# A two-layer encoder on one core: bonus products issued behind the next unit's lta, small weights loaded earlier, one projection block moved forward

## The chip, the core and the metric

The kernel runs on one core of a Trainium2 chip. A core has a matrix engine (TensorE, PE in the profile), a vector engine (VectorE, DVE), an activation engine (ScalarE, ACT), a general engine (GpSimd, POOL) and a sync engine (SyncE, SP) whose queue issues most DMA transfers; ACT's own queue issues some too. Each engine works through its instructions in program order, and the engines wait for each other by semaphores. The metric is the device time of one execution in microseconds (us); lower is better.

## The reference

A sequence of 1280 tokens (one prompt of 256, one sample of 1024) with 1024 channels passes two layers. Layer 0 mixes tokens with a bidirectional RWKV-7 scan, layer 1 with neighbourhood attention; each is followed by a squared-ReLU MLP with 4096 hidden channels. The part that matters here is the preparation of the scan in layer 0:

```python
xw, xa = h + xx * mix[3], h + xx * mix[4]
r, k, v = (h + xx * mix[i]) @ w_rkv[i]      # i = 0, 1, 2
kk = l2_normalised_per_head(k * k_k)
for d in range(2):                          # forward, backward
    w_lora = tanh(xw @ w1[d]) @ w2[d]
    decay = exp(-exp(-softplus(-(w0[d] + w_lora)) - 0.5))
    iclr = sigmoid(a0[d] + (xa @ a1[d]) @ a2[d])
    k_d = k * (1 + (iclr - 1) * k_a)
    y += wkv_scan(r, decay, k_d, v, -kk, kk * iclr, reverse=(d == 1))
    bonus += sum_over_head(r * k_d * r_k)
...
y = groupnorm(y) + bonus * v
out = (y * g) @ w_o
```

All data is float32. The large products are computed as three matmuls each, on operands split into a rounded high part and a rest (high x high, high x low, low x high).

## The kernel before

Channels are tiled in eight blocks of 128, tokens in three segments of 256, 512 and 512. Layer 0 is one stretch of code, `l0_proj`, in these steps.

*Projections.* The norm, the token mixes and the products with `w_k` and with block 0 of `w_r` (receptance) are done first; the results `k_d` and `r_d` go to DRAM. The last result of this step is copied out of PSUM by ACT (L308, kt) and stored by SP (L309).

*Prep stage.* There are 48 units h = 6m + 2s + d, for channel block m, segment s and direction d; the even units are the forward ones. Unit after unit, the following is done:

- `prep_first` (L602): two small matmuls with 64 rows, ltw (decay) and lta (learning rate), from the small weights `wa` of the block. Forward units use the first 64 rows, backward ones the last 64. Each writes a PSUM tile, two buffers of each kind. ACT applies tanh and scalings (L606, L598, L610, L611).
- `prep_scan` (L621, DVE), `prep_exp` (L629 and L632, ACT) and `prep_products` (L649, L655, L663 and L667 on POOL; L651, L657, L659 and L661 on DVE). L657 and L661 read the unit's lta tile last, and with L661 done its bank is free; the ltw bank is free when the scan has read it.
- `prep_keys`, even units only: a 16-row matmul of `heads` (head indicators) with the key norms `kr` into PSUM tile kb (L678), then L681 on DVE.
- `prep_bonus`, even units only: step 0 is a DVE product (L693) that waits for POOL's sum of the two directions (L667), step 1 the bonus matmuls of two columns each, written into the unit's old kb tile (L697), step 2 four DVE copies from there (L703). The next keys matmul but one needs that tile again and waits for the copies.
- `prep_weights`: `wa` of a block, a transfer that ACT's queue issues (L590). `prep_load` (L586): SP loads k (pk), and r of block 0 (pr).

Between these small pieces TensorE is given large work: in blocks 1 to 7 the receptance of the block to come (rps, L96 to L98 by way of `rmm`), and from unit 42 on the values (vps, `v_block`, L516 to L518). Their weights are loaded by SP (`wraw`, L394), cast by ACT (L399) and split by POOL (L400). ACT takes the results out of PSUM (L419 into pr, L522 into vt); both kinds of result share two PSUM buffers. The mixed input of the values is loaded by SP (`vload`, L435), cast by ACT (`vcut`, L439) and split by DVE or POOL (`vlo`, L445).

*What sets the order.* TensorE, DVE, ACT and POOL carry out exactly the order of a list: each piece is put in with a time in units of h, and the list is sorted by it. `lead(t)` stands for max(h + t, -1 + 0.01 h), so that the pieces of the first units gather at -1. A weight's load is at t - 1.988 and its cast at t, both with lower limits. Only SP's queue is ordered by the program's scheduler. At time 52 the scan stage begins, whose first pieces (L837, and L865 copying mt) are mixed in with the last value matmuls. After that come layer 0's output and MLP, the attention layer and its MLP, which take most of the time.

The two lines that set the bonus and the lta in the order:

```python
            at(lead(-0.9), self.prep_first, U, h, 1)
...
                for i, t in enumerate((2.5, 3.0, 3.2)):
                    at(h + t, self.prep_bonus, U, h, i)
```

In unit h, then, the ltw of unit h + 5 comes at h + 2.973, the bonus matmuls of unit h at h + 3.0 and the lta of unit h + 4 at h + 3.1.

Of the kernel before, what the change touches and what calls it, by code (L numbers as in the profile page):

```python
# [5 lines left out]
F32 = mybir.dt.float32  # L6
# [7 lines left out]
P = 128  # L14
# [37 lines left out]
class Trunk:  # L52
# [48 lines left out]
    def l0_proj(self):  # L101
        nc, tc, a = self.nc, self.tc, self.a
# [11 lines left out]
        lp = lctx.enter_context(tc.tile_pool(name="lpA", bufs=1, side="right", reuse_waits="tile"))  # L114
        pre = self.pre = {nm: lp.tile([P, T], F32, name=nm) for nm in ("tw", "ta")}
        pre["kr"] = lp.tile([96, 512], F32, name="kr")
        hctx = ExitStack()
        hp = hctx.enter_context(tc.tile_pool(name="hp", bufs=1, side="right"))
        wk = hctx.enter_context(tc.tile_pool(name="wkA", bufs=2, side="right"))
# [5 lines left out]
        h = hp.tile([P, KT, W], F32, name="h")  # L125
# [65 lines left out]
        def mix_tiles():  # L191
            return [tuple(Pieces(mixp, f"{x}{k}") for x in ("mh", "ml")) for k in range(KT)]
# [154 lines left out]
        while extra:  # L347
            extra.pop(0)()

        w = [self.wsplit(wp, a["w_r"][m], 1024, nc.gpsimd, hb=3, rb=1) for m in range(1)]  # L350
        for s in range(3):
            need(0, s)
# [10 lines left out]
        U = [{} for _ in range(48)]  # L363
        N = 48
        self.cq = []
        at = lambda t, f, *x: self.cq.append((t, len(self.cq), lambda: f(*x)))
        for h in range(N):
            lead = lambda t: max(h + t, -1.0 + 0.01 * h)
            at(lead(-4.633), self.prep_load, U, h)
            at(lead(-2.027), self.prep_first, U, h, 0)  # L370
            at(lead(-0.9), self.prep_first, U, h, 1)
            at(lead(-1.765), self.prep_first, U, h, 2)
            at(lead(-0.65), self.prep_keys, U, h, 0)
            at(lead(-0.2), self.prep_keys, U, h, 1)
            at(lead(-1.1), self.prep_scan, U, h)
            at(lead(-0.693), self.prep_exp, U, h, 0)
            at(lead(-0.69), self.prep_exp, U, h, 1)
            for i, t in enumerate((0.084, 0.415, 0.517, 0.53, 0.54, 0.55, 0.56, 0.57)):
                at(h + t, self.prep_products, U, h, i)
            at(h + 1.191, self.prep_store, U, h, nc.sync)  # L380
            if h % 2 == 0:
                for i, t in enumerate((2.5, 3.0, 3.2)):
                    at(h + t, self.prep_bonus, U, h, i)
            if h % 6 == 0:
                at(max(h + -6.0, -1.5), self.prep_weights, h // 6)
            if h % 6 == 0 and h < 24:
                for i, t in enumerate((0.4, 2.4, 3.4)):
                    at(h + t, self.prep_sigmoid, h // 6, i)
# [12 lines left out]
            wq[key] = hi, lo  # L401

        def weight(key, src, t):
            at(max(t - 1.988, -1.9), wraw, key, src)
            at(max(t, -1.0), wcut, key)
        ev = {}

        def rmm(m, s, k):
# [11 lines left out]
        RL = 4.5  # L420
        for m in range(1, 8):
            for j in range(2):
                weight(("r", m, j), a["w_r"][m, :, 512 * j:512 * j + 512], 6 * m - RL - 2.0 + 0.3 * j)
            for s in range(3):
                for k in range(KT):
                    at(6 * m + 2 * s - RL + 0.25 * k - 0.4, rmm, m, s, k)
                at(6 * m + 2 * s - RL + 1.6, rev, m, s)

        act, vx = mix_tiles(), {}
        VM = 43.3  # L430

        def vload(k, s):
            c0, c1 = SEGS[s]
# [12 lines left out]
        for i, (s, k) in enumerate((s, k) for s in range(3) for k in range(KT)):  # L446
            t = VM + 2 * s - 4 + 0.2 * k
            at(t - 1.9, vload, k, s)
            at(t, vcut, k, s)
            at(t + 0.35, vlo, k, s)  # L450
        VS, VD, VL = 42.5, 0.62, 0.8
        vt = lambda i: VS + VD * i

        def vmm(i):
# [6 lines left out]
        for q in range(4):  # L461
            for j in range(4):
                weight(("v", q, j), a["w_v"][q, :, 2 * j:2 * j + 2, :].rearrange("p k c -> p (k c)"), max(vt(10 * q) - 2.32 + 0.3 * j, vt(10 * q - 1) + 0.01 * j if j > 1 and q else -2.0))
# [64 lines left out]
    def prep_open(self, bctx):  # L528
        nc, tc, a = self.nc, self.tc, self.a
        self.ar_d = self.dram("ar_d", [8, 2, P, 20, P])  # L530
        self.bk_d = self.dram("bk_d", [8, 2, P, 20, P])
        pp = self.pp = bctx.enter_context(tc.tile_pool(name="ppB", bufs=1, reuse_waits="tile", side="right"))
        self.pk = bctx.enter_context(tc.tile_pool(name="pkB", bufs=2, reuse_waits="tile", side="right"))
        self.ppl = bctx.enter_context(tc.tile_pool(name="plB", bufs=2, space=PSUM))
        self.ppn = bctx.enter_context(tc.tile_pool(name="pnB", bufs=2, space=PSUM))
        s = self.pre
        s["ec"] = [[pp.tile([P, 8, 65], F32, name=f"ec{d}{i}") for i in range(2)] for d in range(2)]
        s["raw"] = pp.tile([P, 640], F32, name="l2raw")
        s["m64"] = pp.tile([P, 512], F32, name="m64")
        nc.sync.dma_start(s["m64"], a["m64"])  # L540
        s["hw"] = pp.tile([P, 48], F32, name="hw")
        s["heads"] = pp.tile([96, 1024], F32, name="heads")
        nc.sync.dma_start(s["heads"], a["heads"][0:96])

    def prep_const(self):
        nc, s = self.nc, self.pre
# [242 lines left out]
    def at(self, t, f, level=3):  # L789
        self.todo.append((t, len(self.todo), f, level))  # L790
# [1312 lines left out]
```

## Time and profile before

| | us |
|---|---|
| median of three runs | 3968.65 |
| lowest and highest | 3967.81, 3971.26 |
| the profiled execution | 3964.76 |
| its span | 3963.0 |
| prep stage within the span | about 282 to 645 |

The profile is of one execution. Its granted TensorE clock is 0.977 on average. A row of a timeline gives start and duration in us, engine, line, operation, the tiles out<-in, sizes and how many like it were merged; in brackets stands how long the engine had been idle before it and what ended that. One float32 matmul of the small kind shows as two records, two passes over its columns. A row of windows gives the stretch, its length, the busy time of PE, weight loads, DVE, ACT and POOL, the granted clock, the share of the DMA engines and GB/s.

### The profile page before, as it was taken

What the parts mean: (1) busy time and instruction counts of PE and PEld (TensorE: products, weight loads), DVE (VectorE), ACT (ScalarE), POOL (GpSimd) and SP (SyncE); (2) the same over time, 40 slices, a digit from 0 to 9 for tenths busy, and PEclk for the clock granted to TensorE, in tenths of its full rate; (3) what the DMA queues carried; (4) which work ended last, traced back from release to release, by engine and by line L of the source; (5) the groups of instructions that cost most, each with busy time, mean ns of one, the idle gap of its engine ahead of it and who ended that gap; (6) DMA issues with size and microseconds to landing.
All of it is one profiled execution on the core that took longest, in us unless ns stands there. A gap on an engine that the chain in (4) does not pass through costs nothing.

```text
span 3963.0 us, 89877 instructions
## 1 busy us (share of the span) xinstructions
PE 3751.8 (95%) x36484; PEld 3150.9 (80%) x36484; DVE 2368.9 (60%) x4441; ACT 1684.4 (43%) x4129; POOL 1691.5 (43%) x1541
## 2 busy tenths in 40 slices
PE   8989999888888899999999999999989999999999
PEld 5755579778888788888888889887778788888888
DVE  5777743656565446666666682355563656666666
ACT  6786652555555532222222242456663222222222
POOL 4446652122222424555555561344442455555554
PEclk9989999999999899999999999999999999999999
DMA  3235565666664430111111115444455111111111
GB/s 137 71 105 217 206 227 153 161 164 154 161 152 117 138 115 32 43 40 38 38 43 40 43 64 161 115 108 109 102 146 182 43 35 43 43 41 43 38 40 62
DMA packets 459375, 393.53 MB, mean 99 GB/s; under 512 B 268400, under 2 KB 353520, under 8 KB 458960
## 3 DMA queue, kind: packets, MB, share of 16 engines
q1 hardware_dynamic: 438368, 368.36, 32.3%
q10 hardware_dynamic: 20592, 19.41, 1.5%
q8 instruction: 288, 4.72, 0.5%
q14 instruction: 127, 1.04, 0.1%
HBM read 269.85 MB, written 123.78 MB: 99 GB/s over the span
## 4 chain that ended last, share of the span: by engine, by line
PE 67%; DVE 7%; DMA 5%; ACT 4%; issue 3%; POOL 1%; SPq 1%; ACTq 0%; DVEq 0%; POOLq 0%
PE ps L96 12%; PE ps L97 12%; PE ps L98 12%; PE ps L1491 4%; PE ps L1492 4%; PE ps L1493 4%; PE wu L1009 4%; PE vps L516 1%; PE vps L517 1%; PE vps L518 1%; PE aps L1009 1%; PE op L2015 1%; PE kps L1009 1%; DVE q L878 1%; PE lps L1009 1%
## 5 line engine op out<-in xcount | busy, mean ns | idle before, releaser
L96 PE MATMUL ps<-ah,whi 128*128 128x512 f32 (+1 forms) x2304 | 842.9, 366 | 4.3 <-ACT whi L90 3.3
L98 PE MATMUL ps<-ah,wlo 128*128 128x512 f32 (+1 forms) x2304 | 824.8, 358 | 4.7 <-POOL wlo L91 3.9
L97 PE MATMUL ps<-al,whi 128*128 128x512 f32 (+1 forms) x2304 | 826.2, 359 | 0.0
L96 PEld LDWEIGHTS ps<-ah,whi 128*128 128x128 f32 x2304 | 435.0, 189 | 79.6 <-issue 9.2
L98 PEld LDWEIGHTS ps<-ah,wlo 128*128 128x128 f32 x2304 | 434.0, 188 | 77.4 <-POOL wlo L91 4.5
L97 PEld LDWEIGHTS ps<-al,whi 128*128 128x128 f32 x2304 | 435.2, 189 | 65.6 <-issue 1.0
L1495 DVE TENSOR_TENSOR x<-ps,x 128x512 f32<-128x512 f32 x784 | 484.6, 677 | 0.0
L1399 POOL TENSOR_TENSOR rl<-rl 128x512 f32<-128x512 f32 (+1 forms) x192 | 174.0, 906 | 630.4 <-ACT rl L1398 352.0
L1398 ACT ACTIVATE rl<-ps 128x512 f32<-128x512 f32 (+1 forms) x192 | 101.1, 526 | 793.2 <-PE ps L98 793.2
L91 POOL TENSOR_TENSOR wlo<-raw,whi 128x1024 fp32r<-128x1024 f32 (+1 forms) x113 | 232.8, 2061 | 216.9 <-ACT whi L90 184.0
L1491 PE MATMUL ps<-hhTrue,dh 128*128 128x512 f32 x784 | 307.4, 392 | 1.7 <-DVE x L1495 1.7
L1492 PE MATMUL ps<-hlTrue,dh 128*128 128x512 f32 x784 | 307.4, 392 | 0.0
L1493 PE MATMUL ps<-hhTrue,dl 128*128 128x512 f32 x784 | 306.9, 391 | 0.5 <-POOL dl L1383 0.5
L1383 DVE TENSOR_TENSOR hlTrue<-ts,hhTrue 128x512 fp32r<-128x512 f32 x112 | 133.0, 1187 | 150.0 <-ACT hhTrue L1382 150.0
L1383 POOL TENSOR_TENSOR dl<-raw,dh 128x512 fp32r<-128x512 f32 x128 | 208.8, 1643 | 9.5 <-ACT dh L1382 8.5
L90 ACT CAST whi<-raw 128x1024 fp32r<-128x1024 f32 (+1 forms) x141 | 132.4, 939 | 184.5 <-PE ps L97 77.3
L1506 DVE TENSOR_TENSOR x<-ps,x 128x512 f32<-128x512 f32 x224 | 148.7, 685 | 95.2 <-PE ps L98 93.9
L1383 DVE TENSOR_TENSOR hlTrue<-rl,hhTrue 128x512 fp32r<-128x512 f32 x98 | 88.7, 908 | 185.0 <-ACT hhTrue L1382 184.8
L1382 ACT CAST dh<-ds 128x512 fp32r<-128x512 f32 x112 | 69.3, 619 | 278.5 <-POOL ds L1446 278.5
L1383 POOL TENSOR_TENSOR dl<-ds,dh 128x512 fp32r<-128x512 f32 x112 | 159.1, 1421 | 63.5 <-ACT dh L1382 63.5
L1952 POOL TENSOR_TENSOR s<-s,mx 128x384 f32<-128x384 f32 (+1 forms) x150 | 110.1, 747 | 163.0 <-DVE mx L1951 121.3
L1493 PEld LDWEIGHTS ps<-hhTrue,dl 128*128 128x128 f32 x784 | 147.2, 188 | 33.6 <-POOL dl L1383 1.4
(339 smaller groups left out, 10262.3 us busy)
## 6 DMA issues: line engine op xcount, KB each, us to landing
raw<-in_w_down_dram SPq DMA_DIRECT2D x128, 256.0 KB, 2.8
raw<-in_w_up_dram SPq DMA_DIRECT2D x64, 512.0 KB, 3.4
ar<-ar_d SPq DMA_DIRECT2D x80, 256.0 KB, 3.5
bk<-bk_d SPq DMA_DIRECT2D x80, 256.0 KB, 3.6
ar_d<-ar SPq DMA_DIRECT2D x32, 512.0 KB, 2.7
bk_d<-bk SPq DMA_DIRECT2D x32, 512.0 KB, 3.4
bs<-tab SPq DMA_DIRECT2D x128, 96.0 KB, 3.9
v_d<-vt ACTq DMA_DIRECT2D x80, 128.0 KB, 3.6
```

Of the source, the lines that this page charges most:

```text
L91: lo_eng.tensor_tensor(out=lo[:, cs], in0=raw, in1=hi[:, cs].bitcast(F32), op=ALU.subtract)
L96: mm(ps, sh, mh, start=first, stop=False)
L97: mm(ps, sh, ml, start=False, stop=False)
L98: mm(ps, sl, mh, start=False, stop=last)
L1009: self.nc.tensor.matmul(out, w, x, start=start, stop=stop, skip_group_check=free)
L1383: eng.tensor_tensor(out=lo, in0=src, in1=hi.bitcast(F32), op=ALU.subtract)
L1399: nc.gpsimd.tensor_tensor(out=r, in0=r, in1=r, op=ALU.mult)
L1491: mm(ch[j], hi[:, cs], hh, start=bool(new), stop=False, skip_group_check=True)
L1492: mm(ch[j], hi[:, cs], hl, start=False, stop=False, skip_group_check=True)
L1493: mm(ch[j], lo[:, cs], hh, start=False, stop=True, skip_group_check=True)
L1495: nc.vector.tensor_tensor(out=xv, in0=ch[j], in1=xv, op=ALU.add)
L1506: nc.vector.tensor_tensor(out=xv, in0=ps, in1=xv, op=ALU.add)
```

## The change

- The bonus steps go from (2.5, 3.0, 3.2) to (2.6, 3.12, 3.3). The keys' steps go from -0.65 and -0.2 to -0.55 and -0.15.
- The tiles `heads` and `wa` of block 0 move into a pool that is open earlier, and SP loads them ahead of the first `w_r` block; `prep_weights` is left out for unit 0.
- The limits on weight loads and casts go from -1.9 and -1.0 to -2.3 and -2.2. Block 1's receptance weights are cast at -2.1, and its matmuls and copies are due 5.4 units ahead (4.5 before, and still so in blocks 2 to 7).
- The values' loads, casts and splits come 0.3 units earlier (VM), their copies out of PSUM 0.1 earlier (VL).

```diff
+        pre["heads"] = lp.tile([96, 1024], F32, name="heads")
+        pre["wa", 0] = lp.tile([P, 2, P], F32, name="wa0")
...
+        nc.sync.dma_start(pre["wa", 0], a["wa2"][0])
+        nc.sync.dma_start(pre["heads"], a["heads"][0:96])
         w = [self.wsplit(wp, a["w_r"][m], 1024, nc.gpsimd, hb=3, rb=1) for m in range(1)]
...
-            at(lead(-0.65), self.prep_keys, U, h, 0)
-            at(lead(-0.2), self.prep_keys, U, h, 1)
+            at(lead(-0.55), self.prep_keys, U, h, 0)
+            at(lead(-0.15), self.prep_keys, U, h, 1)
...
-                for i, t in enumerate((2.5, 3.0, 3.2)):
+                for i, t in enumerate((2.6,3.12,3.3)):
                     at(h + t, self.prep_bonus, U, h, i)
-            if h % 6 == 0:
+            if h % 6 == 0 and h:
                 at(max(h + -6.0, -1.5), self.prep_weights, h // 6)
...
-            at(max(t - 1.988, -1.9), wraw, key, src)
-            at(max(t, -1.0), wcut, key)
+            at(max(t - 1.988, -2.3), wraw, key, src)
+            at(max(t, -2.2), wcut, key)
...
-                weight(("r", m, j), a["w_r"][m, :, 512 * j:512 * j + 512], 6 * m - RL - 2.0 + 0.3 * j)
+                weight(("r", m, j), a["w_r"][m, :, 512 * j:512 * j + 512], 6 * m - RL - 2.0 + 0.3 * j if m > 1 else -2.1 + 0.01 * j)
             for s in range(3):
                 for k in range(KT):
-                    at(6 * m + 2 * s - RL + 0.25 * k - 0.4, rmm, m, s, k)
-                at(6 * m + 2 * s - RL + 1.6, rev, m, s)
+                    at(6 * m + 2 * s - (RL if m > 1 else 5.4) + 0.25 * k - 0.4, rmm, m, s, k)
+                at(6 * m + 2 * s - (RL if m > 1 else 5.4) + 1.6, rev, m, s)
...
-        VM = 43.3
+        VM = 43.0
...
-        VS, VD, VL = 42.5, 0.62, 0.8
+        VS, VD, VL = 42.5, 0.62, 0.7
...
-        s["heads"] = pp.tile([96, 1024], F32, name="heads")
-        nc.sync.dma_start(s["heads"], a["heads"][0:96])
```

The line numbers of the kernel after the change are 2 to 4 higher. The order of the instructions on three engines shows what moved.

TensorE in an even unit in the middle of the prep stage, before (ltw, bonus, lta, one group of receptance, keys, receptance):

```order
L602 MATMUL ltw<-tw,wa 128x512
L697 MATMUL kb<-cst,kd 128x2 x4
L602 MATMUL lta<-ta,wa 128x512
L96 MATMUL rps<-mh_192,wh 128x256
L97 MATMUL rps<-ml_195,wh 128x256
L98 MATMUL rps<-mh_192,wl 128x256
L678 MATMUL kb<-kr,heads 128x512
L96 MATMUL rps<-mh_198,wh 128x256
```

The same place in the kernel after:

```order
L604 MATMUL ltw<-tw,wa 128x512
L604 MATMUL lta<-ta,wa 128x512
L96 MATMUL rps<-mh_194,wh 128x256
L97 MATMUL rps<-ml_197,wh 128x256
L98 MATMUL rps<-mh_194,wl 128x256
L699 MATMUL kb<-cst,kd 128x2 x4
L96 MATMUL rps<-mh_200,wh 128x256
L97 MATMUL rps<-ml_203,wh 128x256
L98 MATMUL rps<-mh_200,wl 128x256
L680 MATMUL kb<-kr,heads 128x512
```

The lta has moved ahead of the bonus and stands directly behind the ltw, and one more group of receptance stands between the bonus and the lta. On DVE, L693 (step 0 of the bonus) stands behind L657, L659 and L661 of the same stretch instead of ahead of them. This holds for 21 even units.

ACT at the beginning of the prep stage, before:

```order
L308 COPY kt<-ps 128x512
L590 DMA wa<-in_wa_dram 128x256
L606 ACTIVATE ltw<-ltw,hw 128x256
L598 ACTIVATE ltw<-ltw 128x256
L606 ACTIVATE ltw<-ltw,hw 128x256
L610 ACTIVATE tha<-lta,hw 128x256
L611 ACTIVATE lta<-tha,hw 128x256
L598 ACTIVATE ltw<-ltw 128x256
L629 ACTIVATE ec_3182<-cs 128x4x64
L632 ACTIVATE emc<-cs 128x256
L399 CAST wh<-wraw 128x512 x2
```

The same place in the kernel after:

```order
L310 COPY kt<-ps 128x512
L403 CAST wh<-wraw 128x512 x2
L608 ACTIVATE ltw<-ltw,hw 128x256
L600 ACTIVATE ltw<-ltw 128x256
L608 ACTIVATE ltw<-ltw,hw 128x256
L612 ACTIVATE tha<-lta,hw 128x256
```

The load of `wa` is gone from this place, and the two casts of block 1's first receptance weights have moved ahead of the first tanh.

DVE towards the end of the prep stage (ml is the rest of a value input), before:

```order
L661 SCALAR_TENSOR_TENSOR bk<-lta,emc 128x8x64
L445 TENSOR_TENSOR ml_3237<-vx,mh_3234 128x256
L621 SCALAR_TENSOR_TENSOR cs<-m_3187,ltw 128x256
L703 COPY bonus<-kb 64x4 x4
L651 TENSOR_TENSOR kd<-lta,pk 128x512
```

The same place in the kernel after:

```order
L449 TENSOR_TENSOR ml_3239<-vx,mh_3236 128x256
L663 SCALAR_TENSOR_TENSOR bk<-lta,emc 128x8x64
L695 SCALAR_TENSOR_TENSOR kd<-kd,vec,pr 128x512
L623 SCALAR_TENSOR_TENSOR cs<-m_3191,ltw 128x256
L705 COPY bonus<-kb 64x4 x4
L449 TENSOR_TENSOR ml_3204<-vx,mh_3201 128x512
```

The ml product no longer stands between L661 and the scan. Near the end of the stage ACT's copy of a value block (vt, L522), which stood behind four copies of mt and a weight cast, stands behind two of those copies.

## The prediction

> **What bounds the kernel now.** I read the page first: span, busy time by engine, and the shares of the chain that ended last.
>
> ```profile
> span 3963.0 us, 89877 instructions
> PE 3751.8 (95%) x36484; PEld 3150.9 (80%) x36484; DVE 2368.9 (60%) x4441; ACT 1684.4 (43%) x4129; POOL 1691.5 (43%) x1541
> PE 67%; DVE 7%; DMA 5%; ACT 4%; issue 3%; POOL 1%; SPq 1%; ACTq 0%; DVEq 0%; POOLq 0%
> ```
>
> TensorE is busy for 95% of the span, so an edit pays only where TensorE gets fewer microseconds of work, or waits less. All edits lie in the prep stage, some 280 to 645 us into the span; the rest can only shift. Next I read busy time by windows (columns: window, length, then PE, PEld, DVE, ACT, POOL, granted clock, DMA share, GB/s) and TensorE's waits from 285 to 600 us.
>
> ```profile
> 285.60:302.30 16.70, 16.70 (x42) 8.50 (x43) 10.54 (x19) 11.83 (x25) 8.84 (x12) 0.50 0.81 268
> 360.30:367.10 6.80, 6.80 (x24) 4.68 (x24) 5.22 (x10) 4.06 (x8) 3.94 (x6) 0.50 0.71 251
> 367.55:397.56 30.01, 29.69 (x124) 17.59 (x123) 24.35 (x48) 21.23 (x42) 19.52 (x22) 1.00 0.56 199
> PE ltw L602 <- DMA wa<-in_wa_dram: 3.8, 1, 3.8
> PE kb L678 <- DVE bonus L703: 2.8, 6, 1.5
> ```
>
> The window of 30.01 us is one block (six units) at full clock: TensorE 29.69 us busy, VectorE 24.35. So inside the prep TensorE is the bound, VectorE next at 81%. The other two windows are spells at clock 0.50. The only long wait is the first ltw, 3.8 us for its weights.
>
> **Part 1: bonus behind lta.** In each even unit, before, the small matmuls stood as ltw, bonus, lta. The TensorE timeline (start, duration) shows one such unit, and behind it an odd unit, where no bonus stands between ltw and lta:
>
> ```profile
> 388.48 1.12 PE L602 MATMUL ltw<-tw,wa 64*128 64x512 f32 x2
> 389.64 1.05 PE L697 MATMUL kb<-cst,kd 128*128 128x2 f32 x8
> 390.64 1.12 PE L602 MATMUL lta<-ta,wa 64*128 64x512 f32 x2
> 391.69 0.39 PE L96 MATMUL rps<-mh,wh 128*128 128x256 f32 x1
> 392.58 1.09 PE L678 MATMUL kb<-kr,heads 16*128 16x512 f32 x2 [0.27 <-DVE bonus L703]
> 394.87 0.69 PE L602 MATMUL ltw<-tw,wa 64*128 64x512 f32 x1
> 394.88 0.69 PE L602 MATMUL lta<-ta,wa 64*128 64x512 f32 x1
> 395.93 0.39 PE L96 MATMUL rps<-mh,wh 128*128 128x256 f32 x1
> 396.40 0.28 PE L96 MATMUL rps<-mh,wh 128*128 128x256 f32 x1
> 396.75 0.28 PE L96 MATMUL rps<-mh,wh 128*128 128x256 f32 x1
> ```
>
> In the odd unit ltw and lta start 0.01 us apart and the next work starts at 395.93: both together take 1.06 us. They use 64 rows of the array each, and opposite halves, since ltw of unit h+5 and lta of unit h+4 belong to opposite directions. In the even unit they run one behind the other: lta alone takes 391.69 - 390.64 = 1.05 us. The change puts them side by side there too. The order shows 21 such places: 14 with 512-wide lta and seven with 256-wide lta, for which these rows hold:
>
> ```profile
> 380.05 0.70 PE L602 MATMUL lta<-ta,wa 64*128 64x256 f32 x2
> 380.68 0.50 PE L96 MATMUL rps<-mh,wh 128*128 128x512 f32 x1
> 381.57 0.69 PE L678 MATMUL kb<-kr,heads 16*128 16x256 f32 x2
> 383.00 0.39 PE L96 MATMUL rps<-mh,wh 128*128 128x512 f32 x1
> 383.69 0.39 PE L96 MATMUL rps<-mh,wh 128*128 128x512 f32 x1
> ```
>
> A 256-wide lta costs 0.63. So the lta slots removed are 14 x 1.05 + 7 x 0.63 = 19.1 us. Against this, the receptance matmuls are cut by one more small group: a group of three standing alone takes 381.57 - 380.68 = 0.89 at 512 columns, against 383.69 - 383.00 = 0.69 inside a run, and 392.58 - 0.27 - 391.69 = 0.62 against 0.35 (396.40 to 396.75) at 256. That is 0.20 to 0.27 x 21 = 4.7 us. **TensorE's work shrinks by 14.4 us**, 2.1 per block.
>
> Not all of it need come through, because the earlier lta must find its PSUM bank free: there are two, and lta of unit h+4 waits for VectorE's L661 of unit h+2. These are VectorE's rows:
>
> ```profile
> 387.84 1.75 DVE L693 SCALAR_TENSOR_TENSOR kd<-kd,vec,pr 128x512 f32<-128x512 f32 x1 [3.05 <-POOL kd L667]
> 391.75 0.69 DVE L703 COPY bonus<-kb 64x4 f32<-64x4 f32 x4
> 396.30 0.47 DVE L693 SCALAR_TENSOR_TENSOR kd<-kd,vec,pr 128x256 f32<-128x256 f32 x1
> 397.89 0.68 DVE L661 SCALAR_TENSOR_TENSOR bk<-lta,emc 128x512 f32<-128x512 f32 x1
> ```
>
> The change moves L693 behind L657, L659 and L661, so their 1.2 us fill most of the 3.05 us wait for POOL. At the times of before, L661 would then end well ahead of the pair in the second and third even unit of a block. The next block's first even unit (ltw at 397.56, where the block's window ends) is the narrow place. From the end of the copies at 392.44 to the end of L661 at 398.57 VectorE is busy without a gap for 6.1 us, 5.7 without the L693. After the change TensorE's bonus ends at 388.48 + 1.06 + 0.62 + 1.00 = 391.2 and the copies 0.7 later, so L661 ends near 391.9 + 5.7 = 397.6, while TensorE would reach the pair at 397.56 - 1.05 + 0.27 = 396.8: lta waits about 0.8 us, most of what it gains. The same count for the other two even units (copies and VectorE's work up to the next L661, against TensorE's work up to the next pair) leaves a wait of some 0.25 at the second and none at the third. A block at full clock then takes 30.0 - 2.1 + 0.8 + 0.25 = 29.0. Where a spell slows TensorE the bank is free in time and the 2.1 us come. Seven blocks give 7 (bank late in each) to 14.4 (in none); spells touch about half the blocks, so **I take the middle, -10.5**.
>
> The wait for the copies is the same cover as before: behind the bonus stand one group (0.89 or 0.62) and then the keys, against copies of 0.69 + about 0.2 of handing over: nothing at 512, 0.27 at 256, as before. The new times of the keys and the limits of the casts add no instruction; they are the orders reckoned with here and in part 2.
>
> **Part 2: the start.** Rows of TensorE, ACT, VectorE and the SP queue, the landing of the raw weight tiles (microseconds, all 30 of them), and the window into which the early loads move:
>
> ```profile
> 285.55 1.22 PE L602 MATMUL ltw<-tw,wa 64*128 64x256 f32 x4 [3.82 <-DMA wa<-in_wa_dram]
> 281.81 0.59 ACT L308 COPY kt<-ps 128x512 f32<-128x512 f32 x1 [1.59 <-PE ps L98]
> 286.77 0.45 ACT L606 ACTIVATE ltw<-ltw,hw 128x256 f32<-128x256 f32 x1 [4.38 <-PE ltw L602]
> 287.65 0.69 DVE L621 TENSOR_TENSOR_SCAN cs<-m,ltw 128x256 f32<-128x256 f32 x1 [6.56 <-ACT ltw L598]
> 282.80 0.42 SPq L394 DMA_DIRECT2D wraw<-in_w_r_dram  x1
> DMA to landing us min/median/max: 2.6/3.3/3.6
> 288.67 1.22 PE L602 MATMUL ltw<-tw,wa 64*128 64x512 f32 x1
> 302.99 0.69 PE L602 MATMUL ltw<-tw,wa 64*128 64x512 f32 x1
> 20.00:30.00 10.00, 5.27 (x11) 1.65 (x11) 8.74 (x20) 9.83 (x24) 6.88 (x7) 0.96 0.46 171
> ```
>
> With wa and heads loaded some 255 us earlier (the DMA engines are less than half busy there, so I price those two issues at nothing; without that cover one landing, 2.6 to 3.6 us), the first ltw waits only for ACT's kt copy, which ends at 282.40: 3.1 us earlier. But both casts of the first r weights now stand ahead of the first tanh on ACT. The second waits for a tile issued at 282.80, which lands 2.6 to 3.6 later, 285.4 to 286.4; with a cast of about 0.6 the tanh starts at 286.0 to 287.0, against 286.77. So the 3.8 us go, and a wait for the raw tile is late next. TensorE's next ltw (288.67) follows the scan 1.4 us behind the tanh: 287.5 to 288.5. The work of 288.67 to 302.99 is then the same list in another order; ltw and lta, of which one pair stood apart (289.68 to 293.45), lie side by side, worth 0.8. At half clock it ends near 301.7: -1.3. The 24 receptance groups now follow each other sooner; if full clock returns one or two windows of 3.4 us earlier (the spells in the prep last 3.4 or 6.8), half of that comes back: -3.0 or -4.4. **I take -3.0**, range -0.8 to -4.4.
>
> **Part 3: the end of the prep.** Four waits there, on three engines:
>
> ```profile
> 507.74 1.30 DVE L445 TENSOR_TENSOR ml<-vx,mh 128x256 fp32r<-128x256 f32 x1 [0.47 <-ACT mh L439]
> 510.50 1.14 PE L678 MATMUL kb<-kr,heads 16*128 16x256 f32 x2 [1.49 <-DVE bonus L703]
> 528.69 0.58 PE L516 MATMUL vps<-wh,mh 128*128 128x256 f32 x1 [2.11 <-ACT pr L419]
> 636.01 0.39 PE L516 MATMUL vps<-wh,mh 128*128 128x256 f32 x1 [1.87 <-ACT vt L522]
> ```
>
> The 1.30 us L445 stood ahead of the scan and the copies; the earlier VM puts it before L661, so about 1.4 of the 1.49 goes. At 528.69 ACT's pr copy stood behind the tanh of an lta that came after the bonus: -1.0. At 636.01 ACT's vt copy stood behind four mt copies and a weight cast; two of those and the cast now stand behind it: up to -1.9. Sum 4.3; a later wait on loads (DMA is busiest in this stretch) may take part. **I take -4**, range -1 to -8 (if the half-clock spell of 6.8 us that begins at the 1.49 goes too, 3.4 more).
>
> **Clock.** The five spells from 329 to 493 us cost half their length. They follow the thin stretch (ltw, bonus, lta, the 0.27, keys), yet the same 0.27 at 392.58 caused none, so the phase decides. The thin stretch gets shorter, the bank wait is new: I take 0, range -4 to +2. [...]
>
> **Sum**: -10.5 - 3.0 - 4 + 0 = -17.5. Made against the profiled execution (3964.76 us; span 3963.0) it gives 3947.3; the median of the three runs lies 3.9 above that execution, and I forecast the median: 3968.65 - 17.5 = **3951 us**.
>
> **Rivals.**
> - *The bank gives the time back.* lta waits in every block and each wait starts a spell of one window (1.7 lost): -7 - 3 - 4 + 7 x 1.7 = -2.1, **3967**. For: VectorE's gapless 6.1 us; against: its load of 81%. Chance 0.13. That the pairs don't overlap at all (only the cut groups' +4.7, start and tail) gives 3966 and is in this chance.
> - *All of it comes, and most spells go.* -14.4 - 3 - 4 - 10 (of the 13.5 that 27 us of spells cost): about **3937**. For: the thin stretch is 1 us shorter; against: the unexplained spells. Chance 0.15.
> - *Slower.* The groups between the small matmuls are too thin, and every one of the 21 even units starts a spell: 21 x 1.7 = 36 in place of 13.5, with a keys wait of 0.3 each: +22 + 6 - 17.5 = +11, **3980**. It decides from about ten more spells than today. Against: odd units, with pairs side by side, start none. Chance 0.04. [...]
>
> My forecast has 0.68: 3940 to 3963. **How the numbers follow.** The range for 8 in 10 takes in the lower rival's near side: 3937 to 3965. About 0.2% (7.9 us) is what a measurement of this kernel can tell from no change. Faster than 3960.7: 0.68 x 0.9 + 0.15 = 0.76; slower than 3976.6: 0.04; within: 0.20.
>
> **What would show it.** In the trace after: ltw and lta starting together in even units, and 1.06 us for both; a wait of lta on L661 once a block, up to 0.9; blocks of 28 to 30 us where the clock is full; the first ltw near 282.4 but the first tanh near 286.5; no wait of 1.5 near 500. Wrong would be pairs that start apart, or spells behind most even units.

## The result and the profile after

| | us |
|---|---|
| before, median of five runs | 3967.81 (3963.0 to 3971.26) |
| after, median of five runs | 3946.5 (3945.59 to 3955.96) |
| after / before | 0.9954, 95% interval 0.9939 to 0.9968 |
| forecast | 3951 (3937 to 3965) |

The change makes the kernel 0.5% faster: 21 us by the medians, where 17.5 were forecast. The profiled execution after is the slowest of its five (3955.96 us, span 3954.2), so the two profiles differ by only 8.8 us. The top of its page:

```profile
span 3954.2 us, 89872 instructions
PE 3741.2 (95%) x36484; PEld 3152.9 (80%) x36484; DVE 2372.6 (60%) x4441; ACT 1681.3 (43%) x4129; POOL 1687.0 (43%) x1541
PE 75%; DVE 7%; DMA 6%; ACT 5%; issue 4%; POOL 2%; SPq 1%; ACTq 0%; DVEq 0%; POOLq 0%
```

To see where the time went I cut the prep stage at points that both programs have: the end of the last projection, the keys matmul of unit 4 (the third), that of unit 40, and the last value matmul. The windows (start:end, length, busy PE, PEld, DVE, ACT, POOL, granted clock, DMA share, GB/s) of before:

```profile
281.73:306.53 24.80, 20.98 (x58) 10.74 (x58) 13.49 (x27) 16.41 (x33) 10.03 (x13) 0.66 0.77 254
306.53:498.47 191.94, 190.29 (x734) 112.29 (x733) 151.17 (x291) 131.41 (x250) 119.66 (x138) 0.93 0.59 213
498.47:676.54 178.07, 168.36 (x1270) 149.58 (x1271) 75.95 (x158) 69.46 (x147) 68.62 (x73) 0.94 0.59 182
```

and of after:

```profile
281.86:304.80 22.94, 17.31 (x72) 10.28 (x72) 13.05 (x26) 17.08 (x34) 10.10 (x13) 0.85 0.76 262
304.80:477.50 172.70, 168.88 (x722) 103.60 (x721) 154.17 (x292) 130.50 (x251) 116.78 (x138) 0.97 0.66 236
477.50:656.53 179.03, 170.69 (x1264) 151.28 (x1264) 76.64 (x158) 68.33 (x146) 69.31 (x73) 0.92 0.60 180
361.87:390.87 29.00, 28.42 (x122) 17.56 (x123) 25.91 (x50) 22.22 (x43) 19.41 (x23) 1.00 0.65 233
```

The prep stage is 20.1 us shorter (394.8 to 374.7). Of that 1.9 lie in the start, **19.2 in the six blocks** of the middle, and the end of the stage is 1.0 longer. The blocks hold twelve 512-wide receptance matmuls fewer than before (x722 against x734 on TensorE), because the change does these within the start: four groups of about 0.69, 2.8 us. At equal work the blocks gain some 16 us and the start some 5. The clock gives the second reading. The granted clock in the two traces is either 1.00 or 0.50 (before, 0.50 from 329.64 to 333.05 us and 1.00 from there to 360.36). So time at half clock is 2 x (1 - clock) x length: in the six blocks some 27 us before and 10 after. A block at full clock takes 29.00 (last row) where it took 30.01. Behind the prep stage the program is the same, and its length changes by up to 26 us between the profiled executions of these kernels, for a part that no edit touches; in the profiled execution after it took 11 us of the gain back, while the medians lie as far apart as the two prep stages. So the experiments below are read from the prep stage first and from the times second.

TensorE's timeline after, in an even unit and in the next block's first even unit, with the VectorE rows that belong to the second:

```profile
378.55 0.69 PE L604 MATMUL ltw<-tw,wa 64*128 64x512 f32 x1
378.55 0.69 PE L604 MATMUL lta<-ta,wa 64*128 64x512 f32 x1
380.06 0.95 PE L699 MATMUL kb<-cst,kd 128*128 128x2 f32 x8
381.88 1.09 PE L680 MATMUL kb<-kr,heads 16*128 16x512 f32 x2 [0.42 <-DVE bonus L705]
386.50 1.12 PE L604 MATMUL ltw<-tw,wa 64*128 64x512 f32 x2
387.66 1.12 PE L604 MATMUL lta<-ta,wa 64*128 64x512 f32 x2
386.92 0.68 DVE L663 SCALAR_TENSOR_TENSOR bk<-lta,emc 128x512 f32<-128x512 f32 x1
390.04 0.68 DVE L705 COPY bonus<-kb 64x2 f32<-64x2 f32 x4 [0.92 <-PE kb L699]
```

At 378.55 ltw and lta start together, as forecast. At 386.50 they don't: lta starts at 387.66, just behind the end of L663 (386.92 + 0.68 = 387.60), which frees its bank. No idle time is listed, since ltw fills it, but the side by side is lost there.

### The profile page after: what moved, and what is told of

It is laid out like the page before. It is cut to its first block, busy times and chain, and to the rows that moved or that the text cites. A ratio compares the mean times of both kernels' runs of the same rounds, so it can differ in the third digit from the quotient of the medians.

```text
span 3954.2 us, 89872 instructions
## 1 busy us (share of the span) xinstructions
PE 3741.2 (95%) x36484; PEld 3152.9 (80%) x36484; DVE 2372.6 (60%) x4441; ACT 1681.3 (43%) x4129; POOL 1687.0 (43%) x1541
## 4 chain that ended last, share of the span: by engine, by line
PE 75%; DVE 7%; DMA 6%; ACT 5%; issue 4%; POOL 2%; SPq 1%; ACTq 0%; DVEq 0%; POOLq 0%
PE ps L96 13%; PE ps L97 12%; PE ps L98 12%; PE ps L1493 4%; PE ps L1494 4%; PE ps L1495 4%; PE wu L1011 4%; PE vps L520 1%; PE vps L521 1%; PE vps L522 1%; PE kps L1011 1%; PE op L2017 1%; PE rps L96 1%; PE lps L1011 1%; DMA raw<-in_w_no_dram 1%
```

## The experiments

Every group of runs is compared with the kernel before on the same chip; the medians of that kernel differ by up to 15 us between the chips.

### The parts of the change apart

*Pairs only*: the kernel before with the new times of bonus and keys.

```diff
-                for i, t in enumerate((2.5, 3.0, 3.2)):
+                for i, t in enumerate((2.6, 3.12, 3.3)):
-            at(lead(-0.65), self.prep_keys, U, h, 0)
-            at(lead(-0.2), self.prep_keys, U, h, 1)
+            at(lead(-0.55), self.prep_keys, U, h, 0)
+            at(lead(-0.15), self.prep_keys, U, h, 1)
```

> The kernel before with only the new times of the bonus (2.6, 3.12, 3.3) and of the keys; early loads, casts, block 1's receptance and the values' times stay as before. If the gain comes from lta running beside ltw and from fewer half-clock spells in the blocks: 15 to 17 us below before, about 3952. If it came from the start (small weights early): 0 to 3 us below before, 3965 to 3968.

Measured: 3939.25 us (seven runs, 3935.84 to 3956.57) against 3964.28; ratio 0.9955 (0.9937 to 0.9973). *No pairs*: the changed kernel with these two edits undone.

> The changed kernel with the bonus and the keys at their old times. If the pairs carry the gain: 3 to 6 us below before, 3962 to 3965, first ltw near 282.5 and the start some 4 us shorter. If the start and the tail carry it: 15 to 20 below, under 3953.

Measured: 3964.45 us (twelve runs) against 3964.28; ratio 1.0003 (0.9991 to 1.0015). The windows of the six blocks, of pairs only and then of no pairs, and the start of the latter:

```profile
306.83:483.14 176.31, 172.87 (x733) 106.98 (x733) 155.18 (x293) 130.63 (x252) 116.34 (x138) 0.96 0.64 231
306.16:505.75 199.59, 195.90 (x721) 115.58 (x721) 151.64 (x292) 130.96 (x249) 119.27 (x138) 0.88 0.56 204
281.60:306.16 24.56, 18.57 (x69) 10.51 (x69) 13.48 (x27) 16.92 (x34) 10.20 (x13) 0.79 0.70 242
```

The reordered bonus and keys carry the whole gain that the times can show. Early loads, early casts and value times alone show none, with an interval of about 0.1% to either side. In the profile of no pairs the clock of the blocks even falls to 0.88, 48 us at half clock, and the blocks take 7.7 longer than before. Yet TensorE, VectorE and GpSimd work through these blocks in the order of before, but for the twelve receptance matmuls done earlier. So what stands ahead of the blocks can move their half-clock time by some 20 us.

### Side by side, or only spread out?

The change does two things to the even unit: ltw and lta stand together, and the small matmuls stand apart, with receptance between them. *Unpaired* keeps the second and takes away the first in 18 of 21 places.

```diff
-            at(lead(-0.9), self.prep_first, U, h, 1)
+            at(lead(-0.89 if h % 2 == 0 else -0.9), self.prep_first, U, h, 1)
```

> The changed kernel with one receptance group between ltw and lta in 18 even units (lta of forward units due 0.01 later), so that they no longer run side by side; the bonus stands behind lta and a group between bonus and keys as in the change, with the small matmuls still spread out. If side by side is what pays: the serial lta comes back where the bank was free, 7 to 14 us above the changed kernel. If the spread of the small matmuls and with it the clock is what pays: within 3 us of the changed kernel.

Measured: 3967.41 us (twelve runs) against 3964.28; ratio 1.0012 (1.0002 to 1.0022).

```profile
306.18:505.52 199.34, 196.55 (x721) 113.64 (x721) 153.47 (x292) 131.77 (x251) 116.75 (x138) 0.89 0.56 205
```

One group between ltw and lta costs the whole gain and 44 us at half clock return, so spreading is not what pays. The loss of some 23 us against the change is more than the 7 to 14 of the first theory, as the clock falls too; none of the six blocks is free of half clock, so the profile can't part the serial lta from the clock. *Bonus unsplit* does the reverse: the pair stays and the bonus follows directly, with two receptance groups between it and the keys.

```diff
-                for i, t in enumerate((2.6,3.12,3.3)):
+                for i, t in enumerate((2.6, 3.105, 3.3)):
-        RL = 4.5
+        RL = 4.49
```

> The changed kernel with the bonus directly behind the pair of ltw and lta (receptance 0.01 units later, bonus step 1 at 3.105), so that two receptance groups stand between bonus and keys. If an own receptance group costs 0.2 to 0.27 and the wait of the lta bank follows from the copies behind the bonus: the keys' wait of 0.42 goes, the lta waits of a block's first even unit shrink by some 0.6, and the time falls by 4 to 8 us below the changed kernel. If the products of the bonus (L695) are late there, the bonus itself waits 0.3 or more in each block and the time is the changed kernel's or up to 5 us above it.

Measured: 3945.67 us (five runs) against 3964.28; ratio 0.9957 (0.9942 to 0.9971), the changed kernel's ratio. TensorE's waits from 300 to 480 us, of this kernel and then of the changed one (total, times, longest):

```profile
PE kb L699 <- DVE kd L695: 3.5, 5, 0.9
PE lta L604 <- DVE bk L663: 0.3, 1, 0.3
```

```profile
PE kb L680 <- DVE bonus L705: 2.5, 6, 0.4
PE lta L604 <- DVE bk L663: 0.3, 1, 0.3
```

The keys' wait went, and a wait of the bonus for VectorE's L695 came in its place, as the second theory had it. The group in front of the bonus is therefore no loss: it covers L695.

### Are the half-clock spells luck?

The kernels before and after once more, unchanged.

> The kernel before, for a second profile. The first had 27 us at half clock between 303 and 500 us and 17 at the start; the kernels in which ltw and lta run side by side had 10 to 20, those in which they don't 41 and 44. If the pairs themselves reduce the spells: 25 to 50 us again. If it was the luck of one execution: under 20.

> The changed kernel, for a second profile. If the pairs themselves reduce the spells: 5 to 20 us at half clock between 303 and 500 us, and blocks of 28.6 to 29.0 us where the clock is full. If it was luck: over 25.

The six blocks of the second profile of before and of after (one execution each, 3974.65 and 3960.0 us):

```profile
305.94:497.78 191.84, 190.31 (x734) 112.10 (x733) 151.29 (x292) 131.34 (x250) 119.36 (x138) 0.93 0.59 213
307.48:481.68 174.20, 170.88 (x722) 104.75 (x721) 154.42 (x292) 130.25 (x250) 116.95 (x138) 0.95 0.66 234
```

Before repeats to 0.1 us with the same 27 us at half clock; after has 17 in place of 10. In the first profiles of before and of after the spells of the prep stage begin on a grid of 3.41 us and last a multiple of it. Up to the end of the six blocks they begin, before, at 285.27, 329.64, 360.36, 421.80, 455.94 and 490.07 us, that is 13, 22, 40, 50 and 60 steps behind the first, and last 17.07, 3.41, 6.83, 6.83, 6.83 and 3.41 us; after, at 286.51, 324.06, 354.77 and 412.80, that is 11, 20 and 37 steps behind the first, and last 6.83 and three times 3.41. In the two executions of before the first spell of the blocks lies in the same place against the work: it begins 23.1 and 22.9 us behind their start. The windows of that spell, of the first execution and then of the second:

```profile
329.63:333.04 3.41, 3.41 (x12) 1.68 (x11) 3.41 (x6) 1.33 (x4) 2.67 (x3) 0.50 0.77 259
328.84:332.25 3.41, 3.41 (x12) 1.78 (x11) 3.41 (x7) 1.36 (x3) 2.65 (x3) 0.50 0.79 266
```

So in these two executions the same order, with the first spell in the same place, had the same 27 us. That the place doesn't matter is not shown, and no pairs, with nearly the order of before and 48 us, speaks against it. What speaks for the pairs is the count over all runs told here: the nine profiles of kernels with ltw and lta side by side and single bonus products have 10 to 21 us in these blocks, the four of kernels without pairs 27, 27, 44 and 48. This fits the first theory, but it doesn't say which property of the program it is. *Bonus twice* asks that: the changed kernel issues each bonus product a second time, with the pairs left as they are.

```diff
-            for b in range(nb):
+            for b in (*range(nb), *range(nb)):
```

> The changed kernel with each bonus product issued twice (the second writes the same values again), which adds about 1.0 us of two-column matmuls to each even unit and leaves ltw and lta side by side. If the length of the stretch in which TensorE does only small work brings the half clock: 25 us or more at half clock between the third and the last but three keys matmul (10 and 17 in the changed kernel), and a block some 4 us longer than 29, more than the 2.5 us added. If side by side itself keeps the clock: 10 to 20 us at half clock and blocks of 31 to 31.5.

```profile
307.26:507.38 200.12, 196.30 (x841) 122.29 (x841) 152.72 (x292) 130.53 (x252) 116.85 (x138) 0.89 0.56 204
```

One execution, 3982.96 us, against 3983.89 for one of the kernel before on that chip. The blocks take 200.1 us for 172.7, 27.4 more, of which the added products explain some 15 (2.5 a block). The clock is at 0.89: 44 us at half clock, with TensorE idle no more than 0.41 at a time in five of these six blocks. So side by side alone doesn't keep the clock. More small work per block goes with more half clock, whether it is a serial lta or a doubled bonus, as the first theory had it. With one execution, and 20 us that the work ahead of the blocks can move, this is evidence and not proof.

### The bank that lta waits for

*Bank sooner* puts L663, the last reader of lta, ahead of L661 in every unit.

```diff
-            for i, t in enumerate((0.084, 0.415, 0.517, 0.53, 0.54, 0.55, 0.56, 0.57)):
+            for i, t in enumerate((0.084, 0.415, 0.517, 0.53, 0.54, 0.55, 0.545, 0.57)):
```

> The changed kernel with one exchange on VectorE: L663 (bk, the last reader of the lta tile) ahead of L661 (ar) in every unit, so that the lta bank is free some 0.6 us sooner; nothing else moves on TensorE. If the bank holds back the lta of a block's first even unit: that lta starts about 0.5 us before ltw ends instead of behind it, a block at full clock takes about 28.3 in place of 28.6 to 29.0, and the prep stage gets 2 to 4 us shorter. If something else holds it back: blocks of 28.6 to 29.0 as before and the same time.

Measured: 3962.11 us (twelve runs) against 3978.73; ratio 0.9965 (0.9951 to 0.9978); the changed kernel beside it, with the expectation

> The changed kernel once more on the same chip as the other two, as their measure: 0.994 to 0.996 of the time before.

had 3953.31 (six runs), 0.9946 (0.9928 to 0.9964). Timeline of bank sooner at a block's first even unit:

```profile
391.24 1.12 PE L604 MATMUL ltw<-tw,wa 64*128 64x512 f32 x2
392.17 1.12 PE L604 MATMUL lta<-ta,wa 64*128 64x512 f32 x2
391.43 0.69 DVE L663 SCALAR_TENSOR_TENSOR bk<-lta,emc 128x512 f32<-128x512 f32 x1
```

lta again starts 0.05 us behind the end of L663 (392.12), so the bank does hold it. But it comes free only 0.2 sooner against ltw, not 0.6, and full-clock blocks still take 28.6 to 28.9. What a block at full clock follows now is seen in VectorE's waits over the 29.00 us of the changed kernel:

```profile
DVE bonus L705 <- PE kb L699: 2.7, 3, 1.2
```

25.91 busy and 2.7 waiting for the bonus matmuls make 28.6 of 29.00: VectorE has no other wait in this block. I read TensorE's bonus, VectorE's copies and products, and the lta bank as a loop; moving one product inside it gained nothing.

The time got worse by 8.8 us, and the prep stage with it: 381.9 us, against 372.2 to 376.0 in three profiles of the changed kernel. TensorE waits 6.4 us in its six blocks, in place of 2.8. At 496 us it has a wait of 2.13 of the bonus for L695 that the changed kernel has at 0.16; an ml product of 1.54 now stands between L661 and L695 there:

```profile
493.16 1.54 DVE L449 TENSOR_TENSOR ml<-vx,mh 128x256 fp32r<-128x256 f32 x1
494.62 1.75 DVE L695 SCALAR_TENSOR_TENSOR kd<-kd,vec,pr 128x512 f32<-128x512 f32 x1
```

The rest of the loss was not settled.

### The start and the end of the stage

*Casts late* moves block 1's casts behind the first exps on ACT.

```diff
-                ... if m > 1 else -2.1 + 0.01 * j)
+                ... if m > 1 else -0.6)
```

> The changed kernel with the two casts of block 1's first receptance weights behind the first exps on ACT (due at -0.6), so that the first tanh no longer stands behind the tile issued after r_d. If that wait sets the start: first tanh near 283 in place of 287.6, no wait of 4.9 us of TensorE for the scan, and the next ltw at 285 in place of 289.2; the work up to the first receptance of 512 columns ends 2 to 4 us sooner and the time falls by as much. If the half clock sets it: the same work ends within 1 us of the changed kernel's, since TensorE then does its thin work sooner and at half clock.

Measured: 3954.16 us (five runs) against 3976.22; ratio 0.9944 (0.993 to 0.9957). First the changed kernel's start on PE, ACT and SP, then that of casts late, whose stage begins 1.9 us later:

```profile
289.24 1.22 PE L604 MATMUL ltw<-tw,wa 64*128 64x512 f32 x1 [4.91 <-DVE cs L623]
287.10 0.62 ACT L403 CAST wh<-wraw 128x512 fp32r<-128x512 f32 x1 [1.93 <-DMA wraw<-in_w_r_dram]
287.63 0.44 ACT L608 ACTIVATE ltw<-ltw,hw 128x256 f32<-128x256 f32 x1
282.96 0.38 SPq L398 DMA_DIRECT2D wraw<-in_w_r_dram  x1
```

```profile
285.19 0.45 ACT L608 ACTIVATE ltw<-ltw,hw 128x256 f32<-128x256 f32 x1 [0.79 <-PE ltw L604]
286.82 0.69 PE L604 MATMUL ltw<-tw,wa 64*128 64x512 f32 x1 [0.60 <-DVE cs L623]
283.74:305.32 21.58, 18.56 (x73) 11.08 (x72) 12.97 (x26) 16.88 (x34) 9.98 (x13) 0.84 0.82 277
```

The wait of 4.91 goes, and the start is 1.4 us shorter (21.58 for 22.94; the other two profiles of the changed kernel have 23.64), at or below the low end of the first theory. New waits of TensorE for wh (0.92) and wl (0.77) took the rest. The whole stage takes 371.1 us, against 374.7, 376.0 and 372.2 in three profiles of the changed kernel: not a difference that the times can tell.

*Old tail*: the changed kernel with VM 43.3 and VL 0.8.

```diff
-        VM = 43.0
+        VM = 43.3
-        VS, VD, VL = 42.5, 0.62, 0.7
+        VS, VD, VL = 42.5, 0.62, 0.8
```

> The changed kernel with the old times of the values (VM 43.3, VL 0.8). The waits of TensorE between 480 and 640 us sum to 8.1 us in the changed kernel, and to 9.8 in the one with the pairs alone. If the value times pay as forecast: 3 to 4 us above the changed kernel. If they only move the waits: within 2 us of it.

Measured: 3955.51 us (five runs) against 3976.22; ratio 0.995 (0.9937 to 0.9964), the prep stage 372.1 us. TensorE's waits there sum to over 12 us in place of 8.1, yet the window is 175.0 against 179.0 long, as its clock is 0.97 and not 0.92. So the new value times move waits about, and no gain from them shows. The length of this window goes with the clock: in three profiles of the changed kernel it is 173.1, 178.1 and 179.0 us, at clocks of 0.97, 0.93 and 0.92.

*All three*: the edits of bank sooner, casts late and old tail together, as their diffs show them.

> The changed kernel with the exchange of L663 and L661, the casts of block 1 behind the first exps, and the old times of the values. If these three add up: prep stage 4 to 8 us shorter than the changed kernel's 374 to 376 us, and a time 3 to 8 us below it. If the half-clock spells take back what the start gains: within 2 us of the changed kernel.

Measured: 3961.38 us (twelve runs) against 3978.73; ratio 0.9965 (0.9953 to 0.9976), the stage 377.4 us. They don't add up. No version that was run is better than the change beyond the intervals.

## Why the prediction was right, and where it was not

- **Part 1, the pairs (-10.5): right in mechanism and close in size.** The lta slots go where the bank is free, and the narrow place is the one that was named. The walk gave 29.0 us for a block at full clock; the rows show 28.6 to 29.0, so 1.0 to 1.4 us a block, 7 to 10 over seven. The wait at the narrow place was put at 0.8; there lta loses its whole 1.05. The keys' wait is 0.42, not 0.27.
- **Clock (0, -4 to +2): wrong, and the largest miss.** The step that failed is the price of 0. The prediction saw the thin stretch get shorter, and from one place where the same 0.27 us caused no spell it concluded "so the phase decides". The phase, the place of the 3.41 us grid against the work, may have its part: no pairs has 48 us with nearly the order that has 27 in before, but no run set the place. Yet the profiles with pairs have 10 to 21 us at half clock in the six blocks and those without 27 to 48; for this change 27 became 10 and 17. At equal work some 16 us were gained there, where six times 1.0 to 1.4 make 6 to 8.4; the other 8 to 10 go with the clock. The rival "all of it comes, and most spells go" had this piece right.
- **Why a spell costs less now.** A block with one stretch of 3.4 us at half clock, before and then after:

```profile
306.53:338.06 31.53, 31.21 (x124) 18.29 (x123) 24.89 (x49) 21.87 (x42) 19.99 (x23) 0.95 0.64 229
```

```profile
390.87:420.28 29.41, 28.86 (x122) 18.09 (x123) 25.94 (x50) 21.44 (x42) 19.38 (x23) 0.94 0.64 226
```

  Before it took 1.5 us more than a block at full clock (30.01), after 0.4 more (29.00). As I read it, TensorE is no longer the only bound, and the loop through VectorE has room for part of the slow stretch; no run tests this.
- **Part 2, the start (-3.0): right there, too small to show in the time.** Up to the first 512-wide receptance the work ends at 298.75 in place of 302.99. The tanh came at 287.63, later than the 286.0 to 287.0 forecast: the tile issued at 282.96 let its cast begin at 287.10, 4.1 us later, where I had taken 2.6 to 3.6 for the landing. Full clock returned earlier, at 293.3 in place of 302.3, which covered that:

```profile
286.51:293.34 6.83, 4.10 (x14) 2.61 (x15) 3.15 (x7) 5.49 (x13) 2.80 (x4) 0.50 0.89 292
298.75 0.50 PE L96 MATMUL rps<-mh,wh 128*128 128x512 f32 x1
```

  But pairs only, without these edits, has a stage of 375.4, as long as the changed kernel's 372.2 to 376.0, and the times, good to about 0.2%, can't show 3 us.
- **Part 3, the end (-4): wrong.** Waits of 9.6 us became 8.1 and the window grew by 1.0, at a lower clock. The rows show the step that failed; the last is of pairs only, the others of the changed kernel:

```profile
484.92 0.73 DVE L449 TENSOR_TENSOR ml<-vx,mh 128x256 fp32r<-128x256 f32 x1
485.58 0.68 DVE L663 SCALAR_TENSOR_TENSOR bk<-lta,emc 128x512 f32<-128x512 f32 x1
486.31 0.70 PE L604 MATMUL lta<-ta,wa 64*128 64x256 f32 x2 [1.23 <-DVE bk L663]
509.41 0.58 PE L520 MATMUL vps<-wh,mh 128*128 128x256 f32 x1 [2.21 <-ACT pr L423]
624.05 0.38 PE L521 MATMUL vps<-wl,mh 128*128 128x256 f32 x1 [1.08 <-POOL wl L404]
492.68 0.70 PE L602 MATMUL lta<-ta,wa 64*128 64x256 f32 x2 [2.23 <-DVE bk L661]
```

  The ml product left the way of the copies and stands right ahead of L663, for which lta waits: the 1.49 became 1.23. The wait of lta comes with the pairs; in pairs only, with the old value times, it is 2.23 at this place. I had named the lta bank in part 1 and did not apply it here. The 2.11 stayed, and the 1.87 behind ACT's vt became 1.08 behind POOL's wl and 0.42 behind ACT's cast.
- **The sum.** -17.5 was forecast and about -21 measured. By the profiles the pairs gave 7 to 10 of the 10.5, the clock 8 to 10 that were put at nothing, the start some 4 where 3 were said, and the end nothing of its 4. Errors of opposite sign brought the total near, and that is luck.

## What to carry to other kernels

In this kernel two 64-row matmuls on opposite halves of the array cost one slot (1.06 us at 512 columns) when they stand next to each other, and two (1.16 and 1.05) when another matmul stands between them. Look for such neighbours in the instruction order before shortening anything. Before counting the gain, follow the bank that the earlier matmul must find free: here the vector engine's chain took back one slot in three at full clock. And give half-clock stretches a term of their own in the sum: here they followed the order of the small matmuls (10 to 21 us in the six blocks with pairs, 27 to 48 without), but also what stood ahead (27 and 48 with nearly the same order), so it took several profiles of each kind to see the difference.

## What the runs showed of the hardware

- Half-clock spells in the prep stage of before and of after lie on a grid of 3.41 us and last one to five of its steps (3.41 to 17.07 us). Two executions of before with the first spell of the blocks in the same place against the work (23.1 and 22.9 us behind their start) had the same half-clock time (191.94 and 191.84 us for the six blocks, clock 0.93 both times).
- They need no long idle time. In the 3.4 us ahead of each of the five spells of the blocks of before, TensorE has one wait of 0.27 ahead of four of them, and none ahead of the one at 421.80. With bonus twice TensorE is busy for 196.30 of 200.12 us and the clock is at 0.89; with the pairs it is busy for 168.88 of 172.70 and the clock is at 0.97. The spell at 286.51 of the changed kernel does begin inside a wait, of 4.91 us. More small work goes with more of them in the kernels here (44 us with bonus twice, 10 and 17 in the changed kernel), but it is not all: no pairs has 48 us with nearly the order that has 27 in before. What starts a spell was not shown.
